# Spreading a recurrence's preparation: half of it from GpSimd to VectorE, in spaced steps, held back while the first expert tables are multiplied, and its inputs written to DRAM earlier

## The chip, the cores and the metric

One Trainium2 chip, one of its cores, float32 inputs and outputs, one launch. The metric is the device time of one execution in microseconds, as the median of several runs. Engines are called by two names: TensorE is PE in the profile, VectorE is DVE, ScalarE is ACT, GpSimd is POOL, SyncE is SP.

## The reference

256 tokens of width 2048 pass through two transformer layers. The first has two attention branches with gates, the second an mLSTM branch and a diagonal state-space recurrence (S5). Each ends in an expert layer with 16384 experts, of which each token uses 8 x 16. The expert layer and the recurrence are what matters here:

```python
def block(args):                                  # expert layer, 128 tokens
    xt, it, gt = args
    ue = jnp.take(u_tab, it, axis=0)              # it: 128 experts per token
    ve = jnp.take(v_tab, it, axis=0)
    act = jax.nn.gelu(jnp.einsum('td,ted->te', xt, ue), approximate=False)
    return jnp.einsum('te,ted->td', gt * act, ve)

def s5_groups(u, lam_re, lam_im, log_dt, b_re, b_im, c_re, c_im, d, glu_w):
    dt = jnp.exp(log_dt)[:, None]
    mag = jnp.exp(lam_re * dt)
    ar, ai = mag * jnp.cos(lam_im * dt), mag * jnp.sin(lam_im * dt)
    ...                                           # fr, fi from ar, ai; bbr, bbi = (fr + i fi) * b
    xr = jnp.einsum('bsgh,gph->bsgp', u, bbr)     # 64 groups of 16 channels, 64 states each
    xi = jnp.einsum('bsgh,gph->bsgp', u, bbi)
    _, _, sr, si = lax.associative_scan(combine, (a_r, a_i, xr, xi), axis=1)
    y = einsum(sr, c_re) - einsum(si, c_im) + d * u
    ...                                           # gelu, a 16x32 product, a gate
```

## The kernel before, in words

`program` runs four parts one after the other: `mix1` (the first layer's attention), `peer` (its experts), `mix2` (the second layer's mLSTM and recurrence) and `peer` again.

**The expert layer.** All 16384 experts are computed as dense products, in two halves `r` = 0 and 1. A half has a **u loop** of 64 tiles (u table times tokens, then gelu, then the gates) and a **v loop** of two passes `dh` with 32 tiles each (coefficients times v table). Float32 products are made of three products of split numbers: `weights` loads a tile of 128x2048 on SP's queue (L211), ScalarE rounds it to `w_hi` (L213), VectorE or GpSimd subtracts to get `w_lo` (L219, L217), and `products` (L228) multiplies. `split` (L267, L268) does the same with the coefficients, `coef_hi` and `coef_lo`. There are buffers for two tiles. In the v loops VectorE makes all of `w_lo`.

**Lanes.** `K.bg` holds lanes: Python generators whose instructions are strewn among those of the loops. `K.step(n)` gives n credits; each `yield x` of a lane costs x credits, and a lane goes on while credit is left. `yield 0` waits. Lane instructions on VectorE and GpSimd are ordered behind the newest `w_lo` of that engine. The queue of each engine is set when the program is built, by a planner that follows the order of the program and its own durations; on the chip each engine then works through its queue in order and waits on semaphores.

**The gates** of a half are a lane of their own in the u loop; in the half `r` = 1 GpSimd makes the one-hot matrices for it (L501).

**The preparation.** Behind the u loop of `r` = 0 the first `peer` puts the lane `later` on the list, which is `_s5_prepare`, wrapped in `K.pin`. It computes on VectorE the poles, their powers and a table base, on GpSimd eight rotation tables, and then, in eight **rounds**, two weight matrices w1 and w2 (`expand`, six tensor_tensors of 128x512 each, L1233 to L1235) and a small kernel kc. TensorE transposes the eight blocks of w1 (L1257) and multiplies it with c (L1262), ScalarE copies the transposes back over w1 (L1264), VectorE adds d (L1267), and GpSimd's queue writes w1, kc and w2 to DRAM (L1270, L1271, L1275) and fetches the next round's inputs (L1243, L1245). Each v tile of the first layer gives 2.5 credits, each u tile 1.5 or more.

**The second mixer.** `mix2` first drains the lane if it is not done, then multiplies eight column blocks of u. `u_in` copies each block (ScalarE) to `uT`. `s5_parts(i)` (L1343 to L1351) sends `uT[:, i]` to DRAM, reads it back in another layout as `us`, and reads w1, table and kc, all on SP's queue, on which the weights travel too. `s5_in` (L1360) multiplies, `s5_scan` and `s5_y` follow.

Of the kernel before, what the change touches and what calls it, by code (L numbers as in the profile page):

```python
# [12 lines left out]
P = 128  # L13
# [20 lines left out]
class Ctx:  # L34


    def __init__(self, ctx, tc):
# [32 lines left out]
        self.lo = [None, None]  # L70

# [93 lines left out]
    def pin(self, lane):  # L165

        while True:
            with self.behind(self.lo[0]), self.behind(self.lo[1]):
                took = next(lane, None)
            if took is None:  # L170
                return
            yield took
# [165 lines left out]
def peer(K, wq, keys, u, v, g_out, g_next=None, dst=None, later=None):  # L338
# [208 lines left out]
    for r in range(2):  # L547
        st.update(done=0, groups=0, A=[rp.tile([P, 16, T], F32, name="acts", tag="acts", bufs=4) for _ in range(4)])
        K.bg.append(gates(r, 8 if r else G0))
        for jp in range(NJ // 2):  # L550
            ps = K.ps.tile([P, 2, T], F32, name="ps_u", bufs=2)
            for jj in range(2):
                if jp == NJ // 2 - 1 and jj:
                    K.fine = 3
                w = K.weights(u[r * NJ + jp * 2 + jj], pool=0 if r or ready[0] else UP)
                cols(ps[:, jj], w)
                K.step(1.5 if r else S1 if ready[1] else S0)
            a = st["A"][jp // 8][:, (2 * jp) % 16:(2 * jp) % 16 + 2]
            tg = st["groups"] * TG
            if tg:  # L560
                nc.scalar.activation(ps[:, :, :tg], ps[:, :, :tg], AF.Gelu)
                nc.vector.tensor_tensor(a[:, :, :tg], a[:, :, :tg], ps[:, :, :tg], op=OP.mult)
            if tg < T:
                nc.scalar.activation(a[:, :, tg:], ps[:, :, tg:], AF.Gelu)
            st["done"] = 2 * jp + 2
# [3 lines left out]
        if later is not None:  # L569
            K.bg.append(K.pin(later(rp)))  # L570
            later = None
        end = r == 1
        ext = {}
        for dh in range(2):
# [47 lines left out]
            for jp in range(NJ // 2 - tail):  # L622
                tile_v(jp)(range(TB), range(2))
                K.step(2.5)
# [486 lines left out]
def _s5_prepare(K, I, dram, rp):  # L1111
# [113 lines left out]
    def expand(i, out, a, z, tmp, conj):  # L1225
# [6 lines left out]
        for part, op in ((0, OP.add if conj else OP.subtract), (1, OP.subtract if conj else OP.add)):  # L1232
            g.tensor_tensor(out[:, :, part], aa(0), zz(part), op=OP.mult)  # L1233
            g.tensor_tensor(tm, aa(1), zz(1 - part), op=OP.mult)  # L1234
            g.tensor_tensor(out[:, :, part], out[:, :, part], tm, op=op)  # L1235
# [14 lines left out]
    for i in range(8):  # L1250
        bc, dg = ahead
        expand(i, w1, bc[:, 0], G, spare, True)
        yield 1.2
        for h in range(2):
            ps = K.ps.tile([P, 4, P], F32, name="ps_g", bufs=2)
            for k in range(4):
                nc.tensor.transpose(ps[:, k], flat[:, 4 * h + k], K.ident)  # L1257
            if h == 0:
                kc = K.ps.tile([P, 4, 32], F32, name="ps_g", bufs=2)
                for q in range(4):  # L1260
                    for part in range(2):
                        nc.tensor.matmul(kc[:, q], lhsT=flat[:, 2 * q + part], rhs=bc[:, 1, q, part],  # L1262
                                         start=part == 0, stop=part == 1)
            nc.scalar.copy(flat[:, 4 * h:4 * h + 4], ps)  # L1264
            if h == 0:
                ks = rp.tile([P, 4, 32], F32, name="s5_kc", tag="qT", bufs=2)
                v.tensor_tensor(ks, kc, dg, op=OP.add)  # L1267
        yield 1.2
        expand(i, w2, bc[:, 1], A, spare2, False)
        g.dma_start(dram["w1"][i], W[:, 0])  # L1270
        g.dma_start(dram["kc"][i], ks.rearrange("p q o -> p (q o)"))  # L1271
        if i < 7:
            ahead = inputs(i + 1)
        yield 1.2
        g.dma_start(dram["w2"][i], W[:, 1])  # L1275
        yield 1.2
# [3 lines left out]
def s5_dram(K, ctx):  # L1280
# [3 lines left out]
                u=tile("u", 2, P, T), y=tile("y", 2, P, T), done=False)  # L1284


def mix2(K, I, dram):
# [52 lines left out]
    def s5_parts(i):  # L1340

        j = i % 5
        nc.sync.dma_start(dram["u"][i % 2], uT[:, i])  # L1343
# [3 lines left out]
        for s in range(CH):  # L1347
            rows = slice(32 * s, 32 * s + 32)
            nc.sync.dma_start(us[j][rows], dram["u"][i % 2].rearrange("(q r) (s t) -> s r q t", q=4, s=CH)[s])
# [87 lines left out]
    def u_in(i, ps):  # L1437
        act.copy(uT[:, i].rearrange("p (s c) -> p s c", s=CH), steps(ps))
        if i == 0:
# [376 lines left out]
```

## Time and profile before

| | |
|---|---|
| median of 3 runs | 4207.94 us (4206.15 to 4208.53) |
| profiled execution | 4213.98 us, span 4212.2 us |
| TensorE busy, mean granted clock | 4104.4 us (97%), 0.985 |
| VectorE, ScalarE, GpSimd busy | 2775.9, 2019.9, 1647.6 us |
| L219 (w_lo on VectorE) | 1308 instructions, 1629.0 us |
| L228 (expert and mixer products on TensorE), groups of ps_u<-hT,w_hi alone | 11424 instructions, 1430.0 us |

The profile shows one execution by the hardware profiler. Busy time is that of instructions; the granted clock is TensorE's, as a share of full speed. The releaser of a wait is inferred from semaphore events. Tile names lose their digits in it: `s_work` is `s5_work`, which holds w1 and w2, and `s_prm` holds the poles and the scratch tiles.

### The profile page before, as it was taken

How to read it: one execution, taken by the hardware profiler on the slowest of the kernel's cores; microseconds unless marked ns; L12 is line 12 of the kernel's file. 1: busy time of each engine (PE TensorE's matmuls, PEld its weight loads, DVE VectorE, ACT ScalarE, POOL GpSimd, SP SyncE). 2: the span in 40 equal slices, each digit the busy share in tenths (PEclk: the TensorE clock that was granted, in tenths of full speed). 3: DMA queues.
4: the chain of work that ended last, by engine and by line, in shares of the span. 5: the costliest groups of instructions: out<-in, count | busy, mean ns of one | idle time of the engine just before them, and what ended most of it. 6: DMA issues, size and time to landing. Idle time of an engine off the chain costs nothing. (4 is left out here: it accounts for less than half of the span.)

```text
span 4212.2 us, 74547 instructions
## 1 busy us (share of the span) xinstructions
PE 4104.4 (97%) x29233; PEld 3795.9 (90%) x29233; DVE 2775.9 (66%) x4596; ACT 2019.9 (48%) x2842; POOL 1647.6 (39%) x1370
## 2 busy tenths in 40 slices
PE   8999999999998979999998999999999999999999
PEld 7999989999886779998888998999998889999887
DVE  6775558977777736655557656687765556665565
ACT  5565444444543434444553565544445444444554
POOL 1100016877017967730005451677730007771000
PEclk9999999999999989999998999999999999999999
DMA  5445554555555635555667655555555555555564
GB/s 177 161 151 186 187 182 152 184 188 177 199 197 193 216 130 179 178 185 190 204 205 221 190 167 177 167 166 178 174 184 195 191 195 180 178 178 189 191 205 165
DMA packets 234162, 769.97 MB, mean 183 GB/s; under 512 B 44304, under 2 KB 46352, under 8 KB 233041
## 3 DMA queue, kind: packets, MB, share of 16 engines
q1 hardware_dynamic: 227906, 742.96, 53.7%
q0 software_dynamic: 5904, 22.25, 1.5%
q8 instruction: 229, 3.75, 0.4%
q14 instruction: 123, 1.01, 0.1%
HBM read 748.85 MB, written 16.25 MB: 182 GB/s over the span
## 5 line engine op out<-in xcount | busy, mean ns | idle before, releaser
L219 DVE TENSOR_TENSOR w_lo<-w_raw,w_hi 128x1024 fp32r<-128x1024 f32 (+3 forms) x1308 | 1629.0, 1279 | 1195.9 <-issue 909.9
L213 ACT CAST w_hi<-w_raw 128x1024 fp32r<-128x1024 f32 (+1 forms) x1388 | 1447.1, 1045 | 1589.8 <-PE ps_u L228 615.1
L228 PE MATMUL ps_u<-hT,w_hi 128*128 128x256 f32 x11424 | 1430.0, 282 | 3.7 <-DVE gate L1469 2.1
L228 PEld LDWEIGHTS ps_u<-hT,w_hi 128*128 128x128 f32 x11424 | 1372.9, 189 | 6.6 <-DVE gate L1469 2.4
L501 POOL TENSOR_SCALAR oh<-iota_h,i1T 128x128 f16<-128x128 f16 x896 | 964.9, 1093 | 667.6 <-PE ps_v L228 370.2
L228 PE MATMUL ps_u<-hT,w_lo 128*128 128x256 f32 x5712 | 733.3, 280 | 6.4 <-POOL w_lo L217 6.3
L228 PEld LDWEIGHTS ps_u<-hT,w_lo 128*128 128x128 f32 x5712 | 696.2, 189 | 8.3 <-POOL w_lo L217 7.6
L228 PE MATMUL ps_v<-w_hi,coef_lo 128*128 128x512 f32 x2048 | 690.3, 391 | 9.0 <-DVE coef_lo L268 9.0
L228 PE MATMUL ps_v<-w_hi,coef_hi 128*128 128x512 f32 x2048 | 686.8, 391 | 0.0
L228 PE MATMUL ps_v<-w_lo,coef_hi 128*128 128x512 f32 x2048 | 514.0, 390 | 0.0
L228 PEld LDWEIGHTS ps_v<-w_hi,coef_lo 128*128 128x128 f32 x2048 | 386.1, 189 | 89.3 <-DVE coef_lo L268 9.5
L228 PEld LDWEIGHTS ps_v<-w_hi,coef_hi 128*128 128x128 f32 x2048 | 385.8, 188 | 80.1
L228 PEld LDWEIGHTS ps_v<-w_lo,coef_hi 128*128 128x128 f32 x2048 | 385.0, 188 | 79.9
L217 POOL TENSOR_TENSOR w_lo<-w_raw,w_hi 128x1024 fp32r<-128x1024 f32 (+3 forms) x161 | 309.0, 1933 | 234.3 <-PE ps_u L228 135.5
L267 ACT CAST coef_hi<-acts 128x512 fp32r<-128x512 f32 x256 | 159.5, 624 | 184.6 <-PE ps_v L228 180.2
L268 DVE TENSOR_TENSOR coef_lo<-acts,coef_hi 128x512 fp32r<-128x512 f32 x256 | 193.8, 758 | 0.9 <-ACT coef_hi L267 0.9
L117 POOL TENSOR_TENSOR normed<-x,gain 128x512 f32<-128x512 f32 x22 | 37.7, 1737 | 363.3 <-DVE x L94 276.6
L228 PE MATMUL ps_v<-w_hi,hT 128*128 128x512 f32 (+2 forms) x576 | 127.8, 371 | 1.5 <-ACT hT L267 1.1
L228 PEld LDWEIGHTS ps_v<-w_hi,hT 128*128 128x128 f32 x576 | 101.1, 190 | 20.4 <-ACT hT L267 1.3
L1234 POOL TENSOR_TENSOR s_prm<-s_bc,s_prm 128x512 f32<-128x512 f32 x32 | 41.6, 1303 | 192.6 <-DVE s_prm L1202 191.6
L106 POOL DMA_DIRECT2D gain<-in_final_g x1 | 0.6, 596 | 252.7 <-DVE coef_lo L268 252.7
L106 POOL DMA_DIRECT2D gain<-in_norm_final_g x1 | 0.6, 592 | 252.7 <-DVE coef_lo L268 252.7
(479 smaller groups left out, 3335.6 us busy)
## 6 DMA issues: line engine op xcount, KB each, us to landing
w_raw<-in_p_u SPq DMA_DIRECT2D x512, 512.0 KB, 4.3
w_raw<-in_p_v SPq DMA_DIRECT2D x512, 512.0 KB, 4.2
w_raw<-in_in_gates SPq DMA_DIRECT2D x64, 512.0 KB, 4.2
w_raw<-in_w_out SPq DMA_DIRECT2D x64, 512.0 KB, 4.1
w_raw<-in_p_q SPq DMA_DIRECT2D x48, 512.0 KB, 4.3
w_raw<-in_in_t SPq DMA_DIRECT2D x38, 512.0 KB, 3.8
w_raw<-in_w_ab SPq DMA_DIRECT2D x32, 512.0 KB, 4.4
w_raw<-in_in_qk SPq DMA_DIRECT2D x32, 512.0 KB, 3.9
```

The source lines that it names most:

```text
L106: self.nc.gpsimd.dma_start(gb, bass.AP(tensor=g.tensor, offset=g.offset, ap=[[0, P], [1, D]]))
L117: eng.tensor_tensor(self.normed_cols(tb, c), self.x[:, tb, cc], gb[:, cc], op=OP.mult)
L213: nc.scalar.copy(hi[i], raw[i])
L217: self.lo[1] = nc.gpsimd.tensor_tensor(lo[i][:, m:], raw[i][:, m:], hi[i][:, m:].bitcast(F32), op=OP.subtract)
L219: self.lo[0] = nc.vector.tensor_tensor(lo[i][:, :m], raw[i][:, :m], hi[i][:, :m].bitcast(F32), op=OP.subtract)
L228: self.last_mm = self.nc.tensor.matmul(out, lhsT=a, rhs=b, start=start, stop=stop)
L267: self.nc.scalar.copy(hi, src)
L268: return self.nc.vector.tensor_tensor(lo, src, hi.bitcast(F32), op=OP.subtract)
L501: one = e.tensor_scalar(oh1[:, t], K.iota, i1T[:, t0 + t:t0 + t + 1], None, op0=OP.is_equal)
L1234: g.tensor_tensor(tm, aa(1), zz(1 - part), op=OP.mult)
```

## The change

1. `expand` takes the engine as an argument and yields 0.9 after each instruction. w1 is expanded on VectorE, in six such steps. w2 is expanded on GpSimd, all six instructions at once.
2. The transposes, kc, the copies and the DMAs of a round are spread over four yields of 1, and w1 and kc are written last.
3. `K.hold` is set in each u loop, and `K.pin` yields 0 while it is set.
4. The v loops give 2.0 credits a tile instead of 2.5.
5. In the second mixer `u_in` sends each block to DRAM right behind its copy, into one of eight slots instead of two, and `s5_parts(0)` is called with block 1 instead of block 0.

```diff
@@ Ctx @@
+        self.hold = False
@@ pin @@
         while True:
+            while self.hold:
+                yield 0
             with self.behind(self.lo[0]), self.behind(self.lo[1]):
                 took = next(lane, None)
@@ peer @@
         K.bg.append(gates(r, 8 if r else G0))
+        K.hold = True
         for jp in range(NJ // 2):
...
             K.bg.append(K.pin(later(rp)))
             later = None
+        K.hold = False
...
                 tile_v(jp)(range(TB), range(2))
-                K.step(2.5)
+                K.step(2.0)
@@ _s5_prepare @@
-    def expand(i, out, a, z, tmp, conj):
+    def expand(e, i, out, a, z, tmp, conj):
...
-            g.tensor_tensor(out[:, :, part], aa(0), zz(part), op=OP.mult)
-            g.tensor_tensor(tm, aa(1), zz(1 - part), op=OP.mult)
-            g.tensor_tensor(out[:, :, part], out[:, :, part], tm, op=op)
+            e.tensor_tensor(out[:, :, part], aa(0), zz(part), op=OP.mult)
+            yield 0.9
+            e.tensor_tensor(tm, aa(1), zz(1 - part), op=OP.mult)
+            yield 0.9
+            e.tensor_tensor(out[:, :, part], out[:, :, part], tm, op=op)
+            yield 0.9
...
     for i in range(8):
         bc, dg = ahead
-        expand(i, w1, bc[:, 0], G, spare, True)
-        yield 1.2
-        for h in range(2):
-            ps = K.ps.tile([P, 4, P], F32, name="ps_g", bufs=2)
-            for k in range(4):
-                nc.tensor.transpose(ps[:, k], flat[:, 4 * h + k], K.ident)
-            if h == 0:
-                kc = K.ps.tile([P, 4, 32], F32, name="ps_g", bufs=2)
-                for q in range(4):
-                    for part in range(2):
-                        nc.tensor.matmul(kc[:, q], lhsT=flat[:, 2 * q + part], rhs=bc[:, 1, q, part],
-                                         start=part == 0, stop=part == 1)
-            nc.scalar.copy(flat[:, 4 * h:4 * h + 4], ps)
-            if h == 0:
-                ks = rp.tile([P, 4, 32], F32, name="s5_kc", tag="qT", bufs=2)
-                v.tensor_tensor(ks, kc, dg, op=OP.add)
-        yield 1.2
-        expand(i, w2, bc[:, 1], A, spare2, False)
-        g.dma_start(dram["w1"][i], W[:, 0])
-        g.dma_start(dram["kc"][i], ks.rearrange("p q o -> p (q o)"))
+        yield from expand(v, i, w1, bc[:, 0], G, spare, True)
+        for _ in expand(g, i, w2, bc[:, 1], A, spare2, False):
+            pass
+        yield 1
+        pt = K.ps.tile([P, 4, P], F32, name="ps_g", bufs=2)
+        for k in range(4):
+            nc.tensor.transpose(pt[:, k], flat[:, k], K.ident)
+        kc = K.ps.tile([P, 4, 32], F32, name="ps_g", bufs=2)
+        for q in range(4):
+            for part in range(2):
+                nc.tensor.matmul(kc[:, q], lhsT=flat[:, 2 * q + part], rhs=bc[:, 1, q, part],
+                                 start=part == 0, stop=part == 1)
+        yield 1
+        nc.scalar.copy(flat[:, 0:4], pt)
+        ks = rp.tile([P, 4, 32], F32, name="s5_kc", tag="qT", bufs=2)
+        v.tensor_tensor(ks, kc, dg, op=OP.add)
+        pt = K.ps.tile([P, 4, P], F32, name="ps_g", bufs=2)
+        for k in range(4):
+            nc.tensor.transpose(pt[:, k], flat[:, 4 + k], K.ident)
+        yield 1
+        nc.scalar.copy(flat[:, 4:8], pt)
+        g.dma_start(dram["w2"][i], W[:, 1])
         if i < 7:
             ahead = inputs(i + 1)
-        yield 1.2
-        g.dma_start(dram["w2"][i], W[:, 1])
-        yield 1.2
+        yield 1
+        g.dma_start(dram["w1"][i], flat.rearrange("p n f -> p (n f)"))
+        g.dma_start(dram["kc"][i], ks.rearrange("p q o -> p (q o)"))
@@ s5_dram @@
-                u=tile("u", 2, P, T), y=tile("y", 2, P, T), done=False)
+                u=tile("u", 8, P, T), y=tile("y", 2, P, T), done=False)
@@ mix2 @@
     def s5_parts(i):
...
-        nc.sync.dma_start(dram["u"][i % 2], uT[:, i])
...
-            nc.sync.dma_start(us[j][rows], dram["u"][i % 2].rearrange("(q r) (s t) -> s r q t", q=4, s=CH)[s])
+            nc.sync.dma_start(us[j][rows], dram["u"][i].rearrange("(q r) (s t) -> s r q t", q=4, s=CH)[s])
...
     def u_in(i, ps):
         act.copy(uT[:, i].rearrange("p (s c) -> p s c", s=CH), steps(ps))
-        if i == 0:
+        nc.sync.dma_start(dram["u"][i], uT[:, i])
+        if i == 1:
             s5_parts(0)
```

## Rows read from the trace of the kernel before

**Rows 1.** Stretches of both layers (v loop, then u loop); busy us and instruction counts by engine, and of line L228.
```profile
core 0: us, PE busy (x) PEld busy (x) DVE busy (x) ACT busy (x) POOL busy (x), PEclk, DMA share, GB/s
1061.05:1874.00 812.95, 765.89 (x5314) 698.37 (x5313) 533.13 (x752) 353.45 (x482) 464.92 (x454) 0.96 0.56 184
3128.64:3853.37 724.73, 724.73 (x5123) 663.61 (x5121) 434.95 (x530) 341.28 (x462) 258.96 (x256) 1.00 0.56 186
...
1061.05:1874.00 812.95, 729.72 (x4610) 656.76 (x4609) 0.96 0.56 184
3128.64:3853.37 724.73, 714.53 (x4611) 649.11 (x4609) 1.00 0.56 186
```

**Rows 2.** Stretches of the first layer: ahead of, in and behind the eight rounds; second v loop.
```profile
1061.05:1294.77 233.72, 233.72 (x1034) 193.51 (x1033) 175.91 (x348) 118.65 (x132) 44.06 (x54) 1.00 0.61 203
1294.77:1530.00 235.23, 188.17 (x1027) 162.08 (x1025) 141.60 (x105) 82.87 (x105) 186.91 (x166) 0.87 0.54 177
1530.00:1874.04 344.04, 344.04 (x3258) 342.82 (x3258) 215.65 (x300) 151.93 (x247) 233.95 (x236) 0.99 0.53 175
1874.04:2222.20 348.16, 348.16 (x1538) 288.11 (x1536) 200.48 (x206) 178.91 (x213) 18.94 (x12) 1.00 0.59 197
```

**Rows 3.** Waits of PE from 1300 to 1560 us: total us, times, longest.
```profile
PE ps_g L1257 <- POOL s_work L1235: 35.2, 10, 8.3
PE ps_v L228 <- DVE coef_lo L268: 9.0, 1, 9.0
PE ps_g L517 <- POOL oh L501: 2.9, 4, 1.6
```

**Rows 4.** POOL's instructions by line, 1200 to 1560 us.
```profile
L1235 POOL TENSOR_TENSOR s_work<-s_work,s_prm 128x512 f32<-128x512 f32 x32 | 50.5, 1586 | 0.8
L1233 POOL TENSOR_TENSOR s_work<-s_bc,s_prm 128x512 f32<-128x512 f32 x32 | 42.4, 1337 | 18.3 <-DMA s_bc<-in_s_bc 10.0 <-DMA s_w<-s_work 8.3
L1234 POOL TENSOR_TENSOR s_prm<-s_bc,s_prm 128x512 f32<-128x512 f32 x32 | 41.6, 1303 | 192.6 <-DVE s_prm L1202 191.6
L1270 POOL DMA_DIRECT2D s_w<-s_work x8 | 4.6, 570 | 1.6 <-ACT s_work L1264 1.6
```

**Rows 5.** VectorE's lines L219 and L268 (min/median/max ns): eight rounds, then second layer.
```profile
L219 DVE TENSOR_TENSOR w_lo<-w_raw,w_hi x48: 1210/1636/14755, 1289.3 to 1457.4; 128x1024 fp32r<-128x1024 f32 x48
...
L268 DVE TENSOR_TENSOR coef_lo<-acts,coef_hi x21: 677/1564/1783, 1292.6 to 1436.3; 128x512 fp32r<-128x512 f32 x21
...
L219 DVE TENSOR_TENSOR w_lo<-w_raw,w_hi x121: 1216/1221/1227, 3122.4 to 3449.0; 128x1024 fp32r<-128x1024 f32 x121
...
L268 DVE TENSOR_TENSOR coef_lo<-acts,coef_hi x58: 683/684/686, 3135.7 to 3445.8; 128x512 fp32r<-128x512 f32 x58
```

**Rows 6.** Two short stretches of the eight rounds, columns as in rows 1.
```profile
1340.00:1358.00 18.00, 8.72 (x38) 6.64 (x38) 18.00 (x5) 4.19 (x5) 14.70 (x15) 0.80 0.29 103
...
1400.00:1412.00 12.00, 12.00 (x56) 9.82 (x55) 12.00 (x7) 6.07 (x7) 11.66 (x9) 1.00 0.76 236
```

**Rows 7.** A wait of POOL for a write (1290 to 1560 us), and that write's landing.
```profile
POOL s_work L1233 <- DMA s_w<-s_work: 8.3, 3, 3.4
...
s_w<-s_work POOLq DMA_DIRECT2D x16, 512.0 KB, 3.3
```

**Rows 8.** Timeline of PE, a round's transposes and products at full clock.
```profile
1323.11 0.49 PE L1257 MATMUL ps_g<-ident,s_work 128*128 128x128 f32 x3
1323.44 1.65 PE L1262 MATMUL ps_g<-s_bc,s_work 128*128 128x32 f32 x14
1324.92 0.70 PE L228 MATMUL ps_v<-w_hi,coef_lo 128*128 128x512 f32 x2
```

**Rows 9.** Waits in the second mixer, of SP's queue and of PE.
```profile
SPq L1349 <- DMA s_u<-uT: 3.6, 3, 1.9
...
PE ps_v L1360 <- DMA s_q<-s_u: 2.0, 1, 2.0
```

**Rows 10.** The stretch behind that wait, columns as in rows 1.
```profile
2284.00:2304.00 20.00, 19.48 (x114) 19.51 (x115) 16.21 (x22) 2.29 (x4) 11.17 (x11) 0.66 0.77 234
```

## The prediction, made before the changed kernel ran

> **What bounds the kernel now.** I read the page's slices first, then the stretches, then the waits inside the one that stands out. TensorE is busy 97% of the span, so a microsecond counts only if TensorE idles in it, runs slowly in it or does other work in it. The two expert layers give a yardstick: each runs a v loop (first table half) and then a u loop (second half) over equal tile counts, the first layer with the recurrence's preparation inside, the second without. From the first v product to the first v product of the next half the first layer takes 812.95 us and the second 724.73 us, at TensorE 100% busy and clock 1.00 [rows 1]. The 88.2 us between them are what the preparation costs today. They have three parts. TensorE idles 812.95 - 765.89 = 47.1 us. The L228 products take 729.72 instead of 714.53 us, 15.2 us more (1.4 for each of the eleven long waits below), which goes with the granted clock: 0.96 in the mean, parts of the stretch at the lower of its two levels (1.2 instead of 2.4 GHz). The rest is the preparation's own TensorE work, part of it also at the low clock. All of it lies between 1294.77 and 1530 us: 188.17 busy of 235.23 at clock 0.87, while the stretches ahead of and behind it are busy throughout [rows 2].
>
> Who is waited for: ten waits of the transposes at L1257 for GpSimd's L1235, 35.2 us; one of 9.0 us for VectorE's coef_lo; and 2.9 us for GpSimd's one-hots at L501, which queue behind the preparation on GpSimd [rows 3]. So GpSimd ends last. Its work for one of the eight rounds is 12 tensor_tensors of 134.5/96 = 1.40 us [rows 4] and five DMA issues of about 0.57 us, 19.7 us. The round's yields, 4 x 1.2 = 4.8 credits at 2.5 credits a v tile, cover 1.92 tiles of 5.44 us (348.16/64 [rows 2]), 10.4 us. TensorE's order is fixed beforehand, so it stands at a transpose until GpSimd comes.
>
> The 9.0 us are another thing. A w_lo of VectorE, 1.22 us in the second layer, took 14.755 us once [rows 5], in a stretch in which GpSimd worked almost without a pause (14.70 of 18 us in 15 instructions [rows 6]), and TensorE idled 9.0 us behind it [rows 3]. So 14.76 - 1.22 - 9.0 = 4.5 us of a VectorE standstill are covered by the weight buffers. As a rule the two engines alternate: w_lo takes 1.64 us in the median and coef_lo 1.56 instead of 0.68 [rows 5], with TensorE fully busy all the same while VectorE is at 12.00 of 12 us [rows 6].
>
> **The change part by part.** *Credits.* Up to the eight rounds the yields add up to 99.7 (exponentials 11.7, angles 6, constants 6.6, powers 16.8 + 30.8, table base 10.8, tables 16, first inputs 1). A round now yields 6 x 0.9 + 4 x 1 = 9.4, so all is 174.9. The first half's v loop gives 62 x 2.0 = 124: rounds 0, 1 and the expansions of 2. The hold stops it for the u loop; the remaining 50.9 credits are spent in 26 of the 31 steps of the next half's first v pass. It is done before the norm needs its buffers, and the drain ahead of the second mixer finds nothing.
>
> *GpSimd's share of a round* falls to 6 x 1.40 + 2.9 = 11.3 us, and the round now lasts 9.4/2.0 = 4.7 tiles, 25.6 us. GpSimd has no backlog any more, and no TensorE instruction reads what it computes: w2 only goes to DRAM. The 35.2 us have lost their releaser, and the 2.9 us too, since no preparation runs in the u loop.
>
> *VectorE's share* grows by six tensor_tensors of 128x512 a round. No row shows these on VectorE; the nearest is coef_lo, 128x512 with two SBUF inputs, 0.68 us alone and up to 1.78 us beside GpSimd [rows 5]. I take 0.68 and count contention separately: 4.1 us a round (10.7 at the other end). The tiles need 4.7 x (2 x 1.22 + 0.68) = 14.7 us, s_kc 0.3. Each of the six GpSimd instructions can hold VectorE back once, by about 0.9 us: 5.4. Together 24.5 of 25.6 us. It fits, with little to spare; before, it coped with the same density [rows 6]. The Trainium skill (SBUF — State Buffer, section Who interferes with whom) says that a VectorE instruction with two SBUF inputs and a GpSimd instruction that reads SBUF lock each other out for a whole instruction. By that rule the hold is one GpSimd instruction each time, 6 x 1.40 = 8.4 us, the round would need 27.5 us, 1.9 more than it has, 15 us in all, and with 1.4 us of slow products behind each stall (below) 26: about 4162, which is the first rival below. The usual rows agree with the lock; the 14.755 us, ten times the 1.40 us of a GpSimd instruction, are more than it allows.
>
> *The transposes* are issued a step behind the sixth expansion, and a lane's VectorE work is ordered behind the newest w_lo. By the time TensorE has finished the tile ahead of the transposes, VectorE has had to deliver that tile's w_lo, which is queued behind the expansion. So I set this wait at zero; the other end is the old one, 35.2 us.
>
> *A new wait.* w1 leaves by a GpSimd DMA at the end of a round, and VectorE's first expansion of the next writes the same buffer. Behind it in VectorE's queue stand the next tile's w_lo and coef_lo, for which TensorE waits. The DMA takes 0.58 us to issue and 3.3 us to land; GpSimd used to pay for this, 8.3 us in three waits of up to 3.4 [rows 4, 7]. At 0 to 3.9 us a round this is under the 4.5 us of cover, so it costs nothing unless VectorE is already late. For a few rounds where it is, I take 5 us in all, bounds 0 and 8 x 3.9 = 31.
>
> *TensorE's own work* stays: at full clock three transposes and fourteen products take 1324.92 - 1323.11 = 1.81 us [rows 8]. The records of a round are eight transposes and sixteen products; the five transposes and two products left over are put at 0.65 us by the same pace, which makes 2.46 a round, 19.7 us. The copies on ScalarE, the table arithmetic and the DMAs of the preparation stay in number, and lie beside products.
>
> *The second mixer.* u goes to DRAM as each column block is copied, and eight slots replace two, so the reads no longer stand behind a write on SP's queue. Today SP waits 3.6 us in three places for it and TensorE 2.0 us once [rows 9]. Directly behind, the clock is 0.66 for 20 us [rows 10], worth up to 20 x 0.34 = 6.8 us. What is late next on SP is a write waiting for ScalarE's copy, with weight loads behind it; those are issued two tiles ahead. Bounds: 9 us gained, 5 lost. I take 3 gained, little more than the visible wait, since the short 64-column products that go with the low clock stay. The changed step of 2.0 does nothing in the second layer's v loops, where no lane runs.
>
> **Sum.** 88.2 - 19.7 = 68.5 us return, 5 are given back, 3 come from the mixer: -66.5. The profiled execution took 4213.98 us (span 4212.2), so it would take 4147.5. The median of the runs is 6.0 below it: about 4141 us.
>
> **Rivals.** *VectorE becomes the bound* in the eight rounds. For it: 24.5 of 25.6 us, and the freeze [rows 5]. If a run of six GpSimd instructions freezes it (6 x 1.1 = 6.6 us, 2.1 beyond the cover) or the DMA wait comes on top of a full round (24.5 + 2.5 to 3.9 of 25.6), TensorE loses 1.4 to 2.8 us a round and 1.4 in slow products behind it: 22 to 34 us in the place of the 5, so 4158 to 4170. Against it: one freeze in eight rounds today, with twice the GpSimd work in a row.
>
> *The wait only changes hands*: TensorE's order puts the transposes as far ahead of VectorE as it put them ahead of GpSimd, in other words the change does not do what it says. Then the 68.5 us stay, less the mixer's 3: 4205, no difference. Against it: the queue order above.
>
> *Slower*: VectorE's first expansion waits each round until GpSimd has worked through all it has before the w1 DMA. A standstill of 11.3 + 3.9 = 15.2 us exceeds the cover by 10.7; with 1.4 us of slow products behind each, 8 x 12.1 = 97 us against 71.5 gained: about 4233. It decides from a standstill of 4.5 + 71.5/8 - 1.4 = 12 us a round. Against it: GpSimd has 14 idle us a round, so it should not be behind at that point.
>
> **How the numbers follow.** What can be told from no change is about 0.2%, 8.4 us. Forecast 0.72, by itself 4130 to 4158 (no loss and 9 from the mixer; 18 given back and nothing from it); VectorE bound 0.17; wait changes hands 0.05; slower 0.06. Faster 0.89, same 0.05, slower 0.06. For 8 in 10 the range needs the forecast and most of the second case; with 2 us at the ends for the spread of the runs, 4128 to 4172.
>
> **What would show it.** Right: from the first v product of the first half to the first of the second, about 730 us (724.7 and two rounds of 2.46), TensorE idle under 3 us and clock 1.00; the next v loop about 363 us instead of 348; no wait of L1257 for GpSimd; no preparation between. In the mixer no wait for s_u. Wrong: waits of ps_v products for w_lo or coef_lo, w_lo over 5 us, VectorE's first expansion waiting for the w1 DMA longer than 4.5 us, or transposes waiting for VectorE.

## The result, and the profile after

The changed kernel takes 4154.52 us (median of 4 runs, 4151.97 to 4155.42), the kernel before on the same chip 4207.05 us: a ratio of 0.987, 95% interval 0.9856 to 0.9883. That is 52.5 us less; the forecast was 66 to 67 us less, 4141 us, in a range of 4128 to 4172. The profiled execution took 4154.97 us, span 4153.2, at the kernel's median; that of before lay 6 us above its own.

In the changed file the lines have moved: L228, L219, L268 and L213 are now L231, L222, L271 and L216, the one-hots L501 are L504, the expansions L1233 to L1235 are L1238, L1240 and L1242, the transposes L1266 and L1278.

The stretches that answer to [rows 1, 2] are: first v product to that of the next half in the first layer, the second half's v loop, and the second layer's first-to-second-half stretch. Under them the same first stretch with line L231 alone.

```profile
1061.77:1802.17 740.40, 733.54 (x5170) 670.18 (x5169) 502.80 (x764) 346.38 (x470) 363.39 (x358) 1.00 0.58 192
1802.17:2167.39 365.22, 365.22 (x1681) 303.38 (x1680) 237.15 (x242) 184.85 (x225) 71.31 (x60) 1.00 0.63 207
3069.67:3794.41 724.74, 724.74 (x5123) 663.52 (x5121) 434.93 (x530) 341.58 (x462) 258.99 (x256) 1.00 0.56 186
...
1061.77:1802.17 740.40, 719.34 (x4610) 649.97 (x4609) 1.00 0.58 192
```

The stretch of 812.95 us is now 740.40; the v loop behind it, 347.97 us before, takes 365.22, since most of the preparation moved there (the transposes of six of the eight rounds, VectorE's w1 of five, GpSimd's w2 of four); the second layer is as it was. Together 72.55 - 17.25 = 55.3 us.

TensorE's waits from 1062 to 2170 us are this one row, where [rows 3] had three with 47.1 us:

```profile
PE ps_v L231 <- DVE coef_lo L271: 6.9, 3, 6.2
```

The transposes wait for nobody any more. What is left is one standstill. The windows find it (slices of 50 us), and the timeline shows it (start, duration, in brackets the idle time before and its releaser):

```profile
1300.00:1350.00 50.00, 45.93 (x202) 37.46 (x200) 34.58 (x36) 23.08 (x26) 43.08 (x53) 1.00 0.70 235
1350.00:1400.00 50.00, 47.21 (x211) 38.84 (x212) 41.55 (x37) 21.25 (x24) 22.21 (x19) 0.93 0.62 206
```

```profile
1350.04 0.72 POOL L1221 TENSOR_TENSOR s_work<-s_work,s_prm 128x256 f32<-128x256 f32 x1
1350.79 0.69 DVE L1240 TENSOR_TENSOR s_prm<-s_bc,s_prm 128x512 f32<-128x512 f32 x1 [8.99 <-POOL s_work L1221]
1351.40 0.68 DVE L271 TENSOR_TENSOR coef_lo<-acts,coef_hi 128x512 fp32r<-128x512 f32 x1
...
1352.14 2.08 PE L231 MATMUL ps_v<-w_hi,coef_lo 128*128 128x512 f32 x4 [6.21 <-DVE coef_lo L271]
...
1354.01 0.63 PE L231 MATMUL ps_v<-w_hi,coef_hi 128*128 128x512 f32 x1
...
1356.57 0.42 PE L231 MATMUL ps_v<-w_hi,coef_hi 128*128 128x512 f32 x1
```

In the first round VectorE's second expansion writes a scratch tile that GpSimd is still reading for the last rotation table (L1221). VectorE stands for 8.99 us, the next coef_lo is queued behind it, TensorE idles 6.21 us, and its products then take 0.63 us until 1356.6. So L231 costs 719.34 - 714.53 = 4.8 us more than in the second layer; with the 6.9 us idle, 11.7 us are not got back. Not all of the 4.8 us are slow products behind the standstill. In the next v loop, at clock 1.00 and without any wait, L231 also takes 5.2 us more than in the second layer's v loop:

```profile
1802.17:2167.39 365.22, 353.18 (x1537) 286.80 (x1536) 1.00 0.63 207
3069.67:3417.65 347.98, 347.98 (x1538) 288.11 (x1536) 1.00 0.58 193
```

In the kernel below that has no standstill, L231 takes 717.20 us in the first stretch. By that the slow products are 719.34 - 717.20 = 2.1 us, and 2.7 us go with the rounds: products take longer where the preparation's own stand among them. Why they do was not looked into. GpSimd is late there because a table costs it (14.2 + 15.4 + 16.0 + 4.7 + 4.5)/8 = 6.9 us by the rows below, and its yield of 2 credits covers one v tile of 5.44 us.

```profile
L1221 POOL TENSOR_TENSOR s_work<-s_work,s_prm 128x256 f32<-128x256 f32 x16 | 16.0, 1001 | 0.5
L1220 POOL TENSOR_TENSOR s_prm<-s_work 128x256 f32<-128x256 f32 x16 | 15.4, 961 | 0.6
L1219 POOL TENSOR_TENSOR s_work<-s_work 128x256 f32<-128x256 f32 x16 | 14.2, 903 | 1.7 <-DMA s_tab<-s_work 1.4 <-DVE s_work L1208 0.2
...
L1227 POOL DMA_DIRECT2D s_tab<-s_decay x8 | 4.7, 586 | 0.0
L1226 POOL DMA_DIRECT2D s_tab<-s_work x8 | 4.5, 566 | 1.8 <-POOL s_work L1221 1.8
```

VectorE in the part of the second half's v loop that has the rounds (1802 to 1950 us), where TensorE never waits, by lines, and one of GpSimd's three lines there (the other two also have 8):

```profile
L222 DVE TENSOR_TENSOR w_lo<-w_raw,w_hi 128x1024 fp32r<-128x1024 f32 x50 | 68.8, 1408 | 36.9 <-issue 29.4 <-ACT w_hi L216 7.5
L271 DVE TENSOR_TENSOR coef_lo<-acts,coef_hi 128x512 fp32r<-128x512 f32 x24 | 21.7, 904 | 0.0
L1238 DVE TENSOR_TENSOR s_work<-s_bc,s_prm 128x512 f32<-128x512 f32 x10 | 9.4, 985 | 2.8 <-DMA s_w<-s_work 2.8
L1240 DVE TENSOR_TENSOR s_prm<-s_bc,s_prm 128x512 f32<-128x512 f32 x10 | 6.9, 688 | 0.2
L1242 DVE TENSOR_TENSOR s_work<-s_work,s_prm 128x512 f32<-128x512 f32 x10 | 6.8, 682 | 0.0
...
L1240 POOL TENSOR_TENSOR s_prm<-s_bc,s_prm 128x512 f32<-128x512 f32 x8 | 15.1, 1888 | 0.2
```

Contention with GpSimd, from the mean durations: w_lo 50 x (1.408 - 1.22) = 9.4 us, coef_lo 24 x (0.904 - 0.684) = 5.3 us, the expansions 10 x (0.985 + 0.688 + 0.682) - 30 x 0.68 = 3.1 us. That is 17.8 us beside 24 expansions of GpSimd, the w2 of four rounds: 4.5 us a round.

The mixer (windows from the end of the v loop to the first v product of layer 2), in the kernel before and then in the changed one:

```profile
2222.00:3128.64 906.64, 879.53 (x7186) 854.60 (x7185) 646.10 (x1358) 436.74 (x660) 518.16 (x357) 0.98 0.56 181
```

```profile
2167.39:3069.67 902.28, 875.47 (x7185) 850.40 (x7184) 648.65 (x1358) 437.11 (x660) 519.32 (x357) 0.98 0.56 182
```

The changed kernel's waits of TensorE in that stretch have one row with a new releaser:

```profile
PE ps_g L1414 <- DMA s_yT<-s_y: 2.1, 1, 2.1
```

It is 4.4 us shorter, and TensorE's 2.0 us wait for s_u [rows 9] is gone. But TensorE idles 26.8 us instead of 27.1, as this wait for s_yT, further on in the recurrence, has come in (the same instruction waited 1.3 us for VectorE before) and some others are a little longer; most of the 4.4 us are busy time.

### The profile page after: what moved, and what is told of

Read it like the earlier page. It is cut to its first block, busy times and chain, and to the rows that moved or that the text cites. A ratio compares the mean times of both kernels' runs of the same rounds, so it can differ in the third digit from the quotient of the medians.

```text
span 4153.2 us, 74559 instructions
## 1 busy us (share of the span) xinstructions
PE 4087.2 (98%) x29233; PEld 3780.5 (91%) x29233; DVE 2789.2 (67%) x4644; ACT 2019.0 (49%) x2842; POOL 1595.4 (38%) x1322
## 5 line engine op out<-in xcount | busy, mean ns | idle before, releaser
L222 DVE TENSOR_TENSOR w_lo<-w_raw,w_hi 128x1024 fp32r<-128x1024 f32 (+3 forms) x1308 | 1616.3, 1269 | 1150.8 <-issue 884.5
L216 ACT CAST w_hi<-w_raw 128x1024 fp32r<-128x1024 f32 (+1 forms) x1388 | 1446.9, 1045 | 1586.8 <-PE ps_v L231 625.5
L231 PE MATMUL ps_u<-hT,w_hi 128*128 128x256 f32 x11424 | 1426.3, 281 | 3.2 <-DVE gate L1479 1.7
L231 PEld LDWEIGHTS ps_u<-hT,w_hi 128*128 128x128 f32 x11424 | 1368.8, 188 | 6.3 <-DVE gate L1479 2.0
L504 POOL TENSOR_SCALAR oh<-iota_h,i1T 128x128 f16<-128x128 f16 x896 | 972.4, 1104 | 691.4 <-PE ps_v L231 379.7
L231 PE MATMUL ps_u<-hT,w_lo 128*128 128x256 f32 x5712 | 731.5, 280 | 7.8 <-POOL w_lo L220 6.6
L231 PEld LDWEIGHTS ps_u<-hT,w_lo 128*128 128x128 f32 x5712 | 695.2, 188 | 9.7 <-POOL w_lo L220 7.6
L231 PE MATMUL ps_v<-w_hi,coef_lo 128*128 128x512 f32 x2048 | 693.5, 391 | 6.9 <-DVE coef_lo L271 6.9
L231 PE MATMUL ps_v<-w_hi,coef_hi 128*128 128x512 f32 x2048 | 689.6, 390 | 0.0
L231 PE MATMUL ps_v<-w_lo,coef_hi 128*128 128x512 f32 x2048 | 512.9, 389 | 0.0
L231 PEld LDWEIGHTS ps_v<-w_hi,coef_lo 128*128 128x128 f32 x2048 | 384.5, 188 | 87.9 <-DVE coef_lo L271 8.3
L231 PEld LDWEIGHTS ps_v<-w_hi,coef_hi 128*128 128x128 f32 x2048 | 385.0, 188 | 80.0
L231 PEld LDWEIGHTS ps_v<-w_lo,coef_hi 128*128 128x128 f32 x2048 | 384.2, 188 | 79.8
L271 DVE TENSOR_TENSOR coef_lo<-acts,coef_hi 128x512 fp32r<-128x512 f32 x256 | 188.3, 736 | 0.8 <-ACT coef_hi L270 0.8
L231 PE MATMUL ps_v<-w_hi,hT 128*128 128x512 f32 (+2 forms) x576 | 126.7, 370 | 1.5 <-ACT hT L270 1.1
L231 PEld LDWEIGHTS ps_v<-w_hi,hT 128*128 128x128 f32 x576 | 101.0, 190 | 20.4 <-ACT hT L270 1.3
L1240 POOL TENSOR_TENSOR s_prm<-s_bc,s_prm 128x512 f32<-128x512 f32 x16 | 26.3, 1641 | 234.6 <-DVE s_prm L1207 234.1
L513 DVE TENSOR_TENSOR rh<-oh,g_hi 128x512 f16<-128x512 f16 x128 | 94.5, 738 | 0.1
```

Source lines behind the costliest of these rows:

```text
L216: nc.scalar.copy(hi[i], raw[i])
L222: self.lo[0] = nc.vector.tensor_tensor(lo[i][:, :m], raw[i][:, :m], hi[i][:, :m].bitcast(F32), op=OP.subtract)
L231: self.last_mm = self.nc.tensor.matmul(out, lhsT=a, rhs=b, start=start, stop=stop)
L271: return self.nc.vector.tensor_tensor(lo, src, hi.bitcast(F32), op=OP.subtract)
L504: one = e.tensor_scalar(oh1[:, t], K.iota, i1T[:, t0 + t:t0 + t + 1], None, op0=OP.is_equal)
L513: nc.vector.tensor_tensor(rh, oh2, b2(gh), op=OP.mult)
```

## The experiments

The theory was: the wait for GpSimd at the transposes cost most of what came back; four things removed it together (half the work on another engine, spaced steps, the pause, less work per tile); what is left is the standstill behind the tables; the handling of u brings about 3 us. The rivals were that one of these alone does it, and that others do nothing or harm. Each kernel is compared with before on the same chip, whose median there was 4207.7 to 4210.4 us.

**Only the engine (added to the kernel before).** No spacing, no pause, still 2.5 credits.

```diff
...
-        expand(i, w1, bc[:, 0], G, spare, True)
+        expand(v, i, w1, bc[:, 0], G, spare, True)
...
```

> The kernel before, with only one edit: w1 is expanded on VectorE instead of GpSimd, all six instructions at once as before; no spacing, no pause, 2.5 credits a tile. Theory A: GpSimd's 11.3 us a round nearly fit the 10.4 us of 1.92 tiles, so the transposes no longer wait for it; but VectorE then needs 6.0 us for the tiles, 4.1 for w1, 0.3 and up to 5.4 of contention, 15.8 of 10.4 us, so the wait moves to VectorE's w_lo and coef_lo: some 20 to 45 us of the 68 remain, 4165 to 4190. Rival: the engine is all that matters, and the time is that of the whole change, 4154 within 4 us.

4179.8 us, ratio 0.9928 (0.9913 to 0.9943), inside the range of theory A. Its profiled execution took 4190.62 us, 11 us above the median. Its waits of TensorE from 1062 to 2190 us:

```profile
PE ps_g L1257 <- DVE s_work L1235: 12.5, 5, 5.1
PE ps_v L228 <- DVE coef_lo L268: 11.7, 5, 5.7
```

and two of VectorE's from 1280 to 1560 us:

```profile
DVE s_work L1233 <- DMA s_w<-s_work: 23.0, 6, 6.5
...
DVE s_work L1233 <- POOL s_prm L1215: 10.9, 2, 6.5
```

The engine alone brings some 30 us. Two dangers that the prediction weighed are real here: TensorE waits at the transposes, now for VectorE, and VectorE stands up to 6.5 us for the write of w1, with coef_lo or the transposes behind it. TensorE's longest wait for coef_lo, 5.7 us, is a third thing: it lies behind VectorE's wait for GpSimd's tables (L1215).

**Everything but the engine.** w1 is expanded on GpSimd, in spaced steps and with the pause.

```diff
-        yield from expand(v, i, w1, bc[:, 0], G, spare, True)
+        yield from expand(g, i, w1, bc[:, 0], G, spare, True)
```

> The changed kernel with w1's expansion back on GpSimd; the spacing and the pause stay. Theory A (backlog): GpSimd then has 19.7 us of work in a round of 25.6 us, so it keeps up, the transposes wait for it under 10 us in all, and the time is 4147 to 4160. Rival C (the engine): TensorE's order is set with durations that are too short for GpSimd, so the transposes come too early in every round whatever the spacing: 3 to 8 us in each of eight rounds, 4180 to 4210.

4168.37 us, ratio 0.9902 (0.9884 to 0.992): between the two theories, above the 4160 of A. The transposes' wait, under 10 us by A, is down from ten times to three, but not under 10 us:

```profile
PE ps_g L1266 <- POOL s_work L1242: 14.2, 3, 9.4
```

The timeline of TensorE at the longest:

```profile
1357.44 0.48 PE L1266 MATMUL ps_g<-ident,s_work 128*128 128x128 f32 x1 [9.41 <-POOL s_work L1242]
```

It lies right behind the tables, where GpSimd's backlog now reaches TensorE by way of w1. So everything but the engine gives some 42 us and the engine alone some 30; the whole change gives 52.5, not 72. Both pay off the same wait.

**Without the pause.**

```diff
-        K.hold = True
+        K.hold = False
```

> The changed kernel without the pause in the u loop. Theory A: the pause is worth little or much by GpSimd's load alone. In the u loop the one-hots keep it busy for 36 to 41 of 50 us; a round adds 11.3 us in the 35 us that 9.4 credits take there, 32%, so GpSimd goes over 100%, the one-hots come late and TensorE waits for them: 10 to 40 us more, 4165 to 4195. Rival D: the pause does nothing, since before the change only 2.9 us were waited for one-hots: 4154 within 4 us.

4215.36 us, ratio 1.001 (1.0 to 1.002): the whole gain is gone, which no theory had forecast. TensorE's waits from 1062 to 2230 us, the first row:

```profile
PE ps_g L520 <- POOL oh L504: 35.4, 68, 3.4
```

and the windows at the end of the first layer's u loop:

```profile
1790.00:1830.00 40.00, 25.98 (x247) 22.31 (x245) 32.19 (x54) 8.87 (x13) 39.81 (x43) 0.78 0.42 142
1830.00:1879.00 49.00, 20.71 (x143) 12.43 (x143) 20.62 (x49) 1.76 (x4) 47.57 (x69) 0.50 0.06 23
```

No mark of it inside the loop: GpSimd is less busy there than in the changed kernel (176.60 against 227.95 us from 1450 to 1750). At its end the gates are done in a lump, GpSimd making one-hots without a pause (47.57 of 49 us), TensorE at 20.71 of 49. The loop gives 64 x 1.5 = 96 credits. The gates alone need 32 x (1.8 + 0.9) = 86.4. The spaced preparation has 50.9 left when it gets there, and the two lanes take turns. So 137 want 96, and the loop ends with gates undone. That was a new theory, tested by the next two kernels.

**Without the pause, with more credits in the u loop of the second half,** first in both layers, then in the first layer alone.

```diff
-        K.hold = True
+        K.hold = False
...
-                K.step(1.5 if r else S1 if ready[1] else S0)
+                K.step(2.3 if r else S1 if ready[1] else S0)
```

> The changed kernel without the pause, but with 2.3 credits a tile instead of 1.5 in the u loop of the second half of the table. Theory A (shared credits): the loop now gives 64 x 2.3 = 147 credits, more than the 86.4 of the gates and the 50.9 left of the preparation together, so the gates are no longer done in a lump behind the loop; 4150 to 4172 us, no idle stretch of TensorE from 1750 to 1880 us. Theory B (the preparation and the one-hot matrices get in each other's way on GpSimd and VectorE, whatever the credits are): waits of TensorE for the one-hot matrices stay, now spread over the loop, and the time stays above 4185 us.

4177.85 us, ratio 0.9929 (0.9907 to 0.9951): between the theories, outside both. The first layer behaves as the credits say: the lump is gone, its two stretches take 764.44 + 348.79 us by the first and last v products. The second layer, where no preparation runs, is 20 us slower, 744.5 us instead of 724.7. Its waits of TensorE, and the windows behind its v loop:

```profile
PE ps_g L520 <- POOL oh L504: 12.8, 14, 1.6
```

```profile
3470.00:3520.00 50.00, 47.56 (x447) 46.92 (x447) 32.39 (x45) 20.40 (x45) 47.01 (x50) 0.93 0.47 151
3520.00:3570.00 50.00, 47.49 (x481) 46.83 (x479) 36.19 (x52) 22.98 (x47) 50.00 (x51) 1.00 0.54 173
```

There the gates get all 2.3 credits a tile, which is more one-hots than GpSimd can make: it is busy 47.01 and 50.00 of 50 us, and TensorE waits for it.

```diff
+    shared = later is not None
...
-                K.step(2.3 if r else S1 if ready[1] else S0)
+                K.step((2.3 if shared else 1.5) if r else S1 if ready[1] else S0)
```

> The changed kernel without the pause, with 2.3 credits a u tile in the second half of the first layer's table alone, where the preparation shares the loop with the gates; the second layer keeps 1.5. Theory A (the loss without the pause is that of shared credits, and in the run with 2.3 credits in both layers what was left of it, 23 us, came from the second layer, where the gates alone became too dense for GpSimd's one-hot matrices): second layer's stretch back at 725 us instead of 745, first layer's at 764 as before, 4155 to 4163 us. Theory B (preparation and one-hot matrices get in each other's way whatever the credits): 4170 us or more.

4157.42 us, ratio 0.988 (0.9863 to 0.9897), as the theory of shared credits had it. The second layer's stretch is back at 724.7 us, the first layer's two take 761.1 + 348.8 us, 4 us more together than with the pause. The windows that answer to those of the run without pause:

```profile
1790.00:1830.00 40.00, 40.00 (x347) 38.55 (x346) 24.73 (x36) 18.04 (x27) 14.50 (x18) 1.00 0.51 173
1830.00:1879.00 49.00, 49.00 (x218) 40.59 (x217) 26.71 (x28) 24.66 (x28) 0.00 (x0) 1.00 0.59 195
```

So the pause is worth some 60 us only because the spacing makes the preparation too long for the first half's v loop; it is not that preparation and one-hots hurt each other on GpSimd.

**2.5 credits a v tile instead of 2.0.**

```diff
-                K.step(2.0)
+                K.step(2.5)
```

> The changed kernel with 2.5 credits a v tile as before, so a round has 3.76 tiles, 20.5 us, instead of 25.6. Theory B (VectorE is nearly the bound): its 21.5 us a round no longer fit, 1 us is lost in each round and 1.4 in slow products behind it, 10 to 20 us, 4165 to 4175. Theory A: the time rooms are ample, the standstill of 9 us behind the last table stays, and the time is 4154 within 4 us, or a few us more where the tables come faster than GpSimd makes them (6.9 us of work in 4.35 instead of 5.44).

4163.16 us, ratio 0.9889 (0.9874 to 0.9904): between the two theories (A had 4154 within 4 us or a few us more, B 4165 to 4175). It is 8 to 9 us above the changed kernel by the medians, while the two intervals of the ratio overlap a little. A round then has 9.4/2.5 = 3.76 tiles, 20.5 us. TensorE's waits, and two of VectorE's:

```profile
PE ps_v L231 <- DVE coef_lo L271: 12.2, 5, 5.7
...
PE ps_g L1266 <- DVE s_work L1242: 3.4, 2, 1.8
```

```profile
DVE s_work L1238 <- DMA s_w<-s_work: 11.3, 4, 5.6
DVE s_work L1238 <- POOL s_prm L1220: 10.9, 2, 6.5
```

With less room VectorE is late at the transposes and stands for the write of w1, and coef_lo with it. The second row is the standstill behind the tables again: two of TensorE's five waits for coef_lo, 6.5 of the 12.2 us, lie behind it, and 4.6 us behind the write.

**A scratch tile of its own for the tables,** so that VectorE's second expansion needn't wait for them.

```diff
-        tm = tmp[:, 0].rearrange("p (b x y) -> p b x y", b=4, x=8)
+        tm = own.rearrange("p (b x y) -> p b x y", b=4, x=8)
...
+    own = rp.tile([P, 256], F32, name="s5_own", tag="idx2")
     for i in range(8):
```

> The changed kernel, with one scratch tile of its own for the eight rotation tables on GpSimd; until now they share theirs with w1's expansion on VectorE. Theory A: most of what the change gave back is one standstill, VectorE's second expansion waiting 9.0 us for GpSimd's last table, with 6.2 us of idle TensorE behind it and slow products after. Then that wait is gone, the stretch from the first v product of the first half to that of the second falls from 740.4 to about 731 us, and the time from 4154.5 to about 4145. Rival B: VectorE is simply too full around the rounds (24.5 of 25.6 us a round), so the idle time turns up elsewhere and the time stays at 4154 within 3 us.

4156.08 us, ratio 0.9866 (0.9849 to 0.9882): no gain, theory A missed. The wait moved by one instruction:

```profile
1353.08 0.69 DVE L1239 TENSOR_TENSOR s_work<-s_bc,s_prm 128x512 f32<-128x512 f32 x1 [5.04 <-POOL s_own L1221]
...
1390.01 1.29 DVE L1239 TENSOR_TENSOR s_work<-s_bc,s_prm 128x512 f32<-128x512 f32 x2 [7.67 <-DMA s_w<-s_work]
```

The base of the tables lies in w1's own buffer, so the expansions wait for the last table anyway: not the one tile, but GpSimd's lateness holds them. TensorE idles 4.3 us behind this wait, and 4.8 us more behind the second row, a wait for the write of w1 that the changed kernel has nowhere at this length (its longest is 1.5 us). So this run by itself does not tell the lateness from a VectorE that is too full (rival B, whose time it has); the next one does.

**Room between tables and rounds:** four more credits, two v tiles.

```diff
     ahead = inputs(0)
-    yield 1
+    yield 5
```

> The changed kernel with four credits more (two v tiles, 10.9 us) between the tables and the first round, so that GpSimd has finished the tables, whose scratch and base lie in the tiles that VectorE's first expansions overwrite. The scratch alone did not do it: VectorE's third expansion then waited 5.0 us for the last read of the base. Theory A: both waits go, idle TensorE in the first v loop falls from 6.9 to under 1 us, the stretch from the first v product of the first half to that of the second from 740.4 to 731 plus nothing, and the time by 9 us, to about 4146. Rival B: the idle time turns up in the rounds, 4154 within 3 us.

4152.64 us (4142.69 to 4158.76), ratio 0.9866 (0.9847 to 0.9884). The time is not the 4146 us of theory A but lies in the range of rival B. The trace goes with A: the standstill is gone, TensorE's idle time in the stretch to the next half is 3.3 us instead of 6.9 (A had under 1), the stretch 734.5 us instead of 740.4 (A had 731). TensorE's waits, and line L231 in that stretch:

```profile
PE ps_v L231 <- DVE coef_lo L271: 1.7, 2, 1.2
PE ps_v L231 <- DVE s_decay L1224: 1.6, 1, 1.6
...
1062.47:1796.92 734.45, 717.20 (x4610) 648.36 (x4609) 1.00 0.58 194
```

So the cause of the standstill is shown, and its price is about 6 us in the profile, 3.6 of idle time and 2.1 of slow products; in the runs it can't be told from the changed kernel.

**The handling of u**: the old way in the changed kernel, and then the new way in the kernel before.

```diff
@@ s5_dram @@
-                u=tile("u", 8, P, T), y=tile("y", 2, P, T), done=False)
+                u=tile("u", 2, P, T), y=tile("y", 2, P, T), done=False)
@@ s5_parts @@
+        nc.sync.dma_start(dram["u"][i % 2], uT[:, i])
...
@@ u_in @@
-        nc.sync.dma_start(dram["u"][i], uT[:, i])
-        if i == 1:
+        if i == 0:
             s5_parts(0)
```

> The changed kernel with the second mixer's u handled as before (written in front of its reads, two slots). Theory A: the earlier write is worth the 4.3 us by which the stretch from the end of the first layer's v loop to the first v product of the second layer fell (906.6 to 902.3), so 4158.8. Rival E: that stretch fell because the rest of the program was ordered anew, so it stays at 902 and the time at 4154.5.

4157.27 us, ratio 0.9873 (0.9856 to 0.9889).

> The kernel before, with only the second mixer's edit (u is written right behind its copy, eight slots). Theory E, after the run with the old u handling: the edit is worth nothing that can be told, the mixer's stretch stays between 898 and 907 us and the ratio within 0.2% of 1. Theory A: 4 us, which would be a ratio of 0.999 and a stretch of 902.

4209.61 us, ratio 1.0001 (0.9992 to 1.001). The first kernel's mixer took 897.9 us, 4 us less than the changed kernel's 902.3; the second's took 901.1, 5.5 less than before's 906.6. One comes out for the old way and one for the new, and neither median moves beyond the spread: the edit is worth nothing that these runs can tell.

**Room and the old u together.**

> The changed kernel with four more credits between the last rotation table and the first round (no standstill of VectorE behind the tables), and with u handled as before in the second mixer. Theory A (the two terms add, the gap worth 6 us and the handling of u nothing): 4146 to 4152 us; first v product to first v product of the next half about 734 us, the mixer's stretch within 4 us of that of the changed kernel. Rival (the handling of u was worth the forecast 3 us or more): 4153 us or more, with a wait of TensorE for s_u in the mixer.

4153.3 us, ratio 0.987 (0.985 to 0.989), 0.3 us on the rival's side and well inside the spread of the times (4151.43 to 4156.19), so it decides nothing; the stretch to the next half was 733.3 us as expected. TensorE waited 1.6 us once for s_u, and the mixer took 905.4 us, 7.5 more than in the other kernel with the old u: it varies by that much between kernels that are the same there. No version tried is measurably better than the changed kernel.

## Why the prediction was nearly right

**What bounds, and who is waited for.** Right. The 35.2 us of waits at the transposes are gone, the long freeze behind GpSimd too, and the clock is 1.00 but for the one standstill.

**TensorE's own work** was forecast at 8 x 2.46 = 19.7 us. The six rounds in the v loop cost 365.22 - 347.97 = 17.25, 2.88 each, and 5.2 us of this is L231 itself. The two in the first half: busy outside L231 is 733.54 - 719.34 = 14.2 us, in the second layer 724.73 - 714.53 = 10.2 [rows 1], so 4.0, and 2.7 of L231. Together 23.9, 4.3 over. The term counted the preparation's own instructions alone and put the longer products of the expert layer beside them at nothing. It had given all 15.2 us of them to the low clock; at the v loop's 5.2/6 = 0.87 us a round, an estimate, some 7 of the 15.2 belong to the rounds and stay.

**VectorE's load.** An expansion takes 0.68 us alone as assumed (minimum and median of L1242 agree), and contention is about 4.5 us a round where 5.4 were counted. So a round needs about 14.7 + 4.1 + 0.3 + 4.5 = 23.6 of 25.6 us, close to the forecast's 24.5, and VectorE does not become the bound; with 20.5 us a round it does at the edges, as the run with 2.5 credits shows. The Trainium skill (SBUF — State Buffer, section Who interferes with whom) has the two engines lock each other out for one instruction at a time. After the change the trace agrees: the longest w_lo from 1280 to 2157 us is 2.496 us, so 1.28 over its 1.22, less than one of GpSimd's expansions takes (1.60 us in the mean of 48). By that rule the prediction put six holds of 1.40 us, 8.4 us, into every round; the rows show about 4.5, and the loss worked out from it did not come. Other kernels' traces agree less well (last section).

**The transposes** wait for nobody, as the order of VectorE's queue said.

**The new wait** for the write of w1 is there (5.4 us of VectorE in five places, longest 1.5) and hidden, under the cover of 4.5 us. The runs with less room show its other face, up to 6.5 us and TensorE behind it.

**The steps that were mis-sized** are TensorE's own work, above, and the 5 us "given back". Of the latter, the idle time and the slow products of the first round come to 6.9 + 2.1 = 9.0 us, and their cause was not in the prediction: the first expansions share buffers with the tables, and at 2.0 credits GpSimd ends the tables late. The 5 us stood for another wait, so that they came within a factor of two is luck. The forecast that the wait for GpSimd has no releaser left held for w2 and overlooked that w1, now on VectorE, is bound to GpSimd's tables by memory. Of "TensorE idle under 3 us" 6.9 came.

**The pause** was priced at nothing more than the 2.9 us of one-hots. Without it the whole gain is lost, since the spaced preparation does not fit into the first half. The forecast took the edit as it stood, so its time does not suffer, but this part of the change was not understood. Nor is it so that there is "no preparation between": GpSimd takes up the w2 of two rounds as soon as the one-hots are done, twelve expansions from 1764 to 1787 us, inside the u loop, which ends at 1802. Nobody waits for them.

**The mixer.** 3 us were forecast; the profile shows 4.4, and the experiments disagree on the sign. The wait for s_u went as foreseen: with the old handling TensorE waits 1.6 to 2.0 us once in three of four kernels, with the new one never more than 0.5 us. The wait for s_yT that came is not the edit's doing, since the changed kernel with the old u has it too (1.6 us) and the kernel before with the new u has not. Nothing is shown to be gained.

**The sum.** In the profiles 72.55 - 17.25 + 4.4 us, less 0.7 ahead of the first v product, make the 59.0 us between the spans (4212.2 and 4153.2). The forecast was 66.5; TensorE's own work (4.3 over), the standstill (4.0 over), the mixer (1.4 under) and those 0.7 make up the 7.5, but for rounding. The remaining 6 us of the miss are the offset of before's profiled execution, which was carried over to the changed kernel: its profiled execution lies at its median. One execution above the median is no property of the kernel; before's own times on the chip of the last experiments but one ranged from 4199.28 to 4213.68 us.

## What to carry to other kernels

When background work is fed by credits, spacing it out makes it longer: add up what every lane wants in the loop where it will now land, and either pause one or give more credits there alone. When work moves to another engine, follow its buffers and scratch back to their previous users, for the old engine's lateness comes along through shared memory. Two cures of one wait do not add, so price them together from the wait, not one by one.

## What the runs showed of the hardware

The freeze of VectorE [rows 5] comes back in another kernel. In the kernel before with only u changed, VectorE's next two w_lo again take 15.88 us while GpSimd works through twelve tensor_tensors at 1.05 to 1.28 us each (rows with x2 hold two):

```profile
1334.92 15.88 DVE L219 TENSOR_TENSOR w_lo<-w_raw,w_hi 128x1024 fp32r<-128x1024 f32 x2
1350.72 0.68 DVE L268 TENSOR_TENSOR coef_lo<-acts,coef_hi 128x512 fp32r<-128x512 f32 x1
```

```profile
1335.35 1.09 POOL L1234 TENSOR_TENSOR s_prm<-s_bc,s_prm 128x512 f32<-128x512 f32 x1
1336.40 2.11 POOL L1233 TENSOR_TENSOR s_work<-s_bc,s_prm 128x512 f32<-128x512 f32 x2
...
1347.33 1.25 POOL L1235 TENSOR_TENSOR s_work<-s_work,s_prm 128x512 f32<-128x512 f32 x1
1348.87 0.58 POOL L1275 DMA_DIRECT2D s_w<-s_work  x1 [0.30 <-POOL s_work L1235]
```

VectorE goes on when GpSimd's run ends. In the changed kernel, where GpSimd runs at most five expansions without a break, it did not happen (longest w_lo in these stretches 2.50 us), and GpSimd's expansions take 1.60 us in the mean instead of 1.40. But it takes no run of twelve. With w1 on GpSimd one w_lo of 128x1024 took 4.902 us and another, 32 us later, as long; at 2.5 credits a tile one took 4.793. In each of the three GpSimd had two L1238 and one L1242 without a break:

```profile
L222 DVE TENSOR_TENSOR w_lo<-w_raw,w_hi x33: 1210/2091/4902, 1800.1 to 1900.0; 128x1024 fp32r<-128x1024 f32 x33
```

From 1060 to 2250 us the traces of the thirteen kernels have seven such w_lo that were held for more than 2 us; six of them start while GpSimd issues a DMA with tensor_tensors right behind it. 68 others that start so were held for 1.7 us at most, so that alone does not do it. A hold for one whole instruction is plain elsewhere: at 812.6 us of the changed kernel a w_lo takes 5.62 us, beside one tensor_tensor of GpSimd of 128x2048 that takes 5.33 us. Why the two engines mostly take turns and in some places do not was not settled.
